# A two-layer mixer trunk on one core: gate and output projections of both mixers as seven block products, partners through DRAM

## The chip, the cores and the metric

One core of a Trainium2 chip runs the whole program. The metric is device time in microseconds of one execution; the time before is the median of three runs. In the profile TensorE is PE (its weight loads PEld), VectorE is DVE, ScalarE is ACT, GpSimd is POOL, SyncE is SP.

## What is computed

x is 1 × 1024 tokens × 1024 features, c one conditioning vector. Cut from the reference (layer 0 is gMLP, layer 1 retention, each followed by a squared-ReLU MLP):

```python
def spatial_gating_mixer(h, w_in, ln_g, ln_b, w_s, b_s, w_out):
    z = jax.nn.gelu(h @ w_in);  u, v = jnp.split(z, 2, axis=-1)        # 1024 -> 2 x 2048
    v = layer_norm(v, ln_g, ln_b).reshape(B, nc, CHUNK, SG_GROUPS, SG_GROUP_DIM)
    s = jnp.einsum('gtp,bnpgc->bntgc', jnp.tril(w_s), v) + b_s.T[:, :, None]   # chunks of 128 tokens
    return (u * s.reshape(B, S, SG_WIDTH)) @ w_out                     # 2048 -> 1024

def retention_mixer(h, w_in, gn_g, gn_b, w_out):                       # 4 heads, dk 256, dv 512
    q, k, v, g = jnp.split(h @ w_in, ...)                              # 1024, 1024, 2048, 2048
    o = chunkwise_retention(rotary(q), rotary(k) * RET_DK ** -0.5, v)  # a state per head, chunks of 128
    o = ((o - mu) * lax.rsqrt(var + 1e-5)) * gn_g + gn_b
    return (o * jax.nn.silu(g)) @ w_out                                # 2048 -> 1024

for i in range(2):
    mod = silu(c) @ ada_w[i] + ada_b[i]                                # shift, scale, gate for mixer and MLP
    h = rms_norm(x, pre_mix_g[i]) * (1 + scale_m) + shift_m
    x = x + gate_m * rms_norm(mixer(h), post_mix_g[i])
    h = rms_norm(x, pre_ffn_g[i]) * (1 + scale_f) + shift_f
    y = jnp.square(jax.nn.relu(h @ ffn_w_in[i])) @ ffn_w_out[i]        # 1024 -> 4096 -> 1024
    x = x + gate_f * rms_norm(y, post_ffn_g[i])
```

## The kernel before

The tokens are two streams a = 0, 1 of 512. h is kept feature-major (128 features × 512 tokens a tile, eight tiles a stream). Every operand is split into a high and a low part, `hi` + `lo`, and one product is three matmuls, hi·hi, hi·lo and lo·hi (`mm3`, L132 to L134). So each weight tile of 128 × 1024 costs ScalarE a cast (`hi`, L345) and VectorE a subtraction, the remainder (`lo`, L351); activations likewise.

Work is a list of items `It`, each with `fetch` (the weights' DMA on SP), `prep` (`hi` and `lo`) and `run` (24 matmuls of 512 columns, as a rule); single functions, the pieces, stand between items. The loop at the end of the file (`advance`) fetches and prepares up to AHEAD = 5 items ahead, as far as W_BUFS = 6 weight tiles and other caps let it; within that a scheduler sets each engine's order.

- `feat_items` (two items) makes 256 output features for one stream, `tok_items` (four items) 512 output features with tokens on partitions; `plain_items` and `out_items` are second factors for one stream, adding to `step.y` (`Step.add`, L727).
- `block_items` makes 256 features for **both** streams in seven products in place of eight (a 2 × 2 block scheme over the halves of the contraction, of the columns and the streams): per product 4 × 3 matmuls, 84 where plain takes 96. Its weights' sums are L458 to L463, the remainders L475, sums of the results L498. `seven_items` is the same for the second factor, per 512 rows of contraction 168 matmuls for 192, with weights' sums L594 to L600, remainders L613, and activations read back from DRAM (`zd`) and split (L558, L562). `Parts.put` makes the sums of activations for it (L527 to L530).
- `Ops` makes the streams' sums that the products of `block_items` need. Stream 0's h goes to DRAM (`hd`), stream 1's stays on chip; `sums` (L846 to L854) are spread over the eight items of stream 1's plain blocks.
- Only the two MLPs use this scheme (`ffn_items`): FIRST = 4 plain blocks of 16 for stream 0 and for stream 1, then 12 blocks in seven products, then the second factor. During the first stretch (eight items) the norm of the mixer's stream 1 runs as pieces: `Step.finish` loads, sums squares (L201) and multiplies by the gate (L749), updates x (L761), makes the factors; then the scaled rows (L781), the tiles' transposes (L225) and the affine to h (L698, L703, L704).
- The mixers go stream by stream: `sg_items(step, h)` makes v, its layer norm, then in turn u (`u_items`), the spatial product (`s_bg`, L1064, L1065: the high part against both parts of w_s in one matmul of 256 columns, the low part in one of 128; VectorE L1069 to L1071), and the output projection. `ret_items(step, h)` goes by heads: q, k, v, scores, then per chunk o, kv and an item of g; transposes of o, gate (L1240), projection.
- adaLN vectors are items too (`ada_items`: VectorE L287, L289), put between others by `spread`.

Of the kernel before, what the change touches and what calls it, by code (L numbers as in the profile page):

```python
# [8 lines left out]
F32 = mybir.dt.float32  # L9
# [4 lines left out]
P = 128  # L14
# [17 lines left out]
AHEAD = 5  # L32

# [23 lines left out]
def kernel(  # L57
# [200 lines left out]
    class It:  # L258
# [141 lines left out]
    def out_items(step, w, r0, zt, zahead=2):  # L400

        st, zp = {}, {}

        def zpre():
            for j in range(2):
                zp[j] = split2(zt[j], "zp")

        def fn(W, l, j):
            if j == 0:
                st["ps"] = [PW(), PW()]  # L410
            if j == 0:
# [14 lines left out]
        its[0].zpre, its[0].zahead = zpre, zahead
        return its

# [80 lines left out]
    class Parts:  # L509
# [6 lines left out]
        def __init__(self, key):  # L516
            self.key, self.seven, self.four = key, {}, {}

        def put(self, b, z1, z2):
# [14 lines left out]
            nc.gpsimd.dma_start(d[:, 5:7], sb)  # L534

# [30 lines left out]
    def seven_items(two, w, parts, pairs):  # L566
# [9 lines left out]
        def item(p, g):  # L576
# [66 lines left out]
            return It(run, fetch, (hi, lo), w=2, raw=raws, rel=2 * (p in (7, 4)), z=1, zrel=1, cap=OUT_CAP)  # L643
# [3 lines left out]
    def plain_items(step, w, parts, blocks):  # L647
# [4 lines left out]
        def fn(W, l, j):  # L652
# [12 lines left out]
            if l == 1:  # L665
                st.pop(("z", j))

# [13 lines left out]
    class H:  # L681
# [8 lines left out]
        def split(self, d, src, layer, ffn, first=False, keep=None):  # L690
# [8 lines left out]
            tmp = keep(d) if keep else G()  # L699
# [7 lines left out]
    class Step:  # L707
# [21 lines left out]
        def finish(self):  # L729
# [11 lines left out]
            def sums():  # L741
                ss = small(8)
                for t in range(NCH):
                    for l in range(2):
                        square_sum(y[t // 2, l][0][:, t % 2, :], ss[:, 2 * t + l : 2 * t + l + 1])
                for l in range(2):
                    for i in range(2):
                        yt = y[i, l][0]
                        nc.vector.tensor_tensor(  # L749
                            yt, yt, st["g"][:, l, :][:, None, :].broadcast_to([P, 2, 512]), ALU.mult  # L750
                        )
                st["r"] = row_rsqrt(row_mean(ss))
                st["ss"] = small(8)
# [21 lines left out]
            return [load, sums, update(0), update(1)] + ([] if self.ends else [factors])  # L775
# [12 lines left out]
    def reload(a, l, xs):  # L788

        for i in range(2):  # L790
            xs[i, l] = QH("xr")
            nc.sync.dma_start(xs[i, l], rows_of(xsrc[a], i, l))

# [6 lines left out]
    def reload_pieces(a, tile_):  # L800
# [756 lines left out]
```

## Time and profile before

| | |
|---|---|
| median of three runs | 2787.8 us (2787.01 to 2788.74) |
| the profiled execution | 2788.15 us, span 2786.4 us |
| TensorE busy | 2727.5 us (98%), 12360 matmuls and transposes |
| VectorE busy | 1835.2 us (66%) |
| ScalarE busy | 1236.6 us (44%) |
| GpSimd busy | 120.4 us (4%) |

Read it so: TensorE's share says that the time is made of matmuls; whether a matmul removed is time gained depends on whether its stretch has TensorE without gaps, so the next thing to read is the stretches, then the few rows in which TensorE waited and for whom.

### The profile page before, as it was taken

How to read it: one execution, taken by the hardware profiler on the slowest of the kernel's cores; microseconds unless marked ns; L12 is line 12 of the kernel's file. 1: busy time of each engine (PE TensorE's matmuls, PEld its weight loads, DVE VectorE, ACT ScalarE, POOL GpSimd, SP SyncE). 2: the span in 40 equal slices, each digit the busy share in tenths (PEclk: the TensorE clock that was granted, in tenths of full speed). 3: DMA queues.
4: the chain of work that ended last, by engine and by line, in shares of the span. 5: the costliest groups of instructions: out<-in, count | busy, mean ns of one | idle time of the engine just before them, and what ended most of it. 6: DMA issues, size and time to landing. Idle time of an engine off the chain costs nothing.

```text
span 2786.4 us, 32308 instructions
## 1 busy us (share of the span) xinstructions
PE 2727.5 (98%) x12360; PEld 2249.1 (81%) x12360; DVE 1835.2 (66%) x2459; ACT 1236.6 (44%) x1755; POOL 120.4 (4%) x206
## 2 busy tenths in 40 slices
PE   6999999999999999999999999999999999999997
PEld 5887878888887888887888888888888888888886
DVE  7775745677787777747655557655556766677745
ACT  4443433347555643344433335433427555564322
POOL 0000000001101000000000000000001001100000
PEclk9999999999999999999999999999999999999998
DMA  9632452256566554445213215323226545475433
GB/s 355 224 114 76 151 182 91 91 174 200 180 222 218 208 189 158 137 152 195 91 61 110 73 59 190 128 84 116 78 65 218 167 164 181 143 254 168 146 124 121
DMA packets 253419, 421.97 MB, mean 151 GB/s; under 512 B 14064, under 2 KB 113592, under 8 KB 253264
## 3 DMA queue, kind: packets, MB, share of 16 engines
q1 hardware_dynamic: 236816, 363.17, 39.9%
q0 software_dynamic: 16256, 56.67, 5.3%
q8 instruction: 97, 1.59, 0.2%
q14 instruction: 58, 0.48, 0.1%
q10 hardware_dynamic: 192, 0.07, 0.0%
HBM read 346.43 MB, written 73.42 MB: 151 GB/s over the span
## 4 chain that ended last, share of the span: by engine, by line
PE 87%; issue 6%; DVE 3%; DMA 2%; POOL 1%; ACT 1%; POOLq 0%; ACTq 0%; DVEq 0%; SPq 0%
PE ps L132 17%; PE ps L133 17%; PE ps L134 17%; PE pw L132 12%; PE pw L134 12%; PE pw L133 12%; DMA first<-in_ada_w_dram 1%; PE ps L225 1%; DVE w L351 1%; DMA raw<-in_sg_w_in_dram 1%; PE ps L1229 0%; DVE x L761 0%; DMA raw<-in_ada_w_dram 0%; DVE y L749 0%; PE ps L1064 0%
## 5 line engine op out<-in xcount | busy, mean ns | idle before, releaser
L132 PE MATMUL ps<-h,w 128*128 128x512 f32 x1696 | 664.7, 392 | 10.3 <-DVE g L1070 8.6
L134 PE MATMUL ps<-h,w 128*128 128x512 f32 x1696 | 663.8, 391 | 0.0
L133 PE MATMUL ps<-h,w 128*128 128x512 f32 x1696 | 663.3, 391 | 0.0
L351 DVE TENSOR_TENSOR w<-raw,w 128x1024 fp32r<-128x1024 f32 (+1 forms) x296 | 355.3, 1208 | 406.9 <-PE ps L133 164.4
L345 ACT CAST w<-raw 128x1024 fp32r<-128x1024 f32 (+1 forms) x296 | 303.9, 1035 | 569.5 <-PE pw L134 178.8
L132 PEld LDWEIGHTS ps<-h,w 128*128 128x128 f32 x1696 | 318.9, 188 | 79.5 <-issue 6.5
L133 PEld LDWEIGHTS ps<-h,w 128*128 128x128 f32 x1696 | 319.1, 188 | 67.5
L134 PEld LDWEIGHTS ps<-h,w 128*128 128x128 f32 x1696 | 318.8, 188 | 67.8
L132 PE MATMUL pw<-w,z 128*128 128x512 f32 x640 | 249.7, 390 | 0.0
L133 PE MATMUL pw<-w,z 128*128 128x512 f32 x640 | 249.0, 389 | 0.0
L134 PE MATMUL pw<-w,z 128*128 128x512 f32 x640 | 247.8, 389 | 0.0
L132 PE MATMUL pw<-w,zp 128*128 128x512 f32 x512 | 201.5, 394 | 0.0
L133 PE MATMUL pw<-w,zp 128*128 128x512 f32 x512 | 199.5, 390 | 0.2 <-DVE w L351 0.2
L134 PE MATMUL pw<-w,zp 128*128 128x512 f32 x512 | 198.4, 391 | 0.8 <-DVE zp L139 0.8
L613 DVE TENSOR_TENSOR w<-raw,w 128x1024 fp32r<-128x1024 f32 x84 | 102.8, 1223 | 89.3 <-issue 32.8
L558 ACT CAST z<-zraw 128x1024 fp32r<-128x1024 f32 x100 | 104.7, 1051 | 114.7 <-DVE z L562 91.2
L727 DVE TENSOR_TENSOR y<-y,pw 128x1024 f32<-128x1024 f32 x100 | 121.5, 1216 | 48.5 <-PE pw L134 48.5
L132 PEld LDWEIGHTS pw<-w,z 128*128 128x128 f32 x640 | 120.1, 188 | 26.2 <-DVE y L727 1.6
L134 PEld LDWEIGHTS pw<-w,z 128*128 128x128 f32 x640 | 120.2, 188 | 25.1
L133 PEld LDWEIGHTS pw<-w,z 128*128 128x128 f32 x640 | 120.2, 188 | 24.6
L608 ACT CAST w<-raw 128x1024 fp32r<-128x1024 f32 x84 | 88.2, 1051 | 114.6 <-PE pw L134 48.1
L562 DVE TENSOR_TENSOR z<-zraw,z 128x1024 fp32r<-128x1024 f32 x100 | 121.3, 1219 | 2.8 <-ACT z L558 2.8
(218 smaller groups left out, 4455.0 us busy)
## 6 DMA issues: line engine op xcount, KB each, us to landing
zraw<-zd SPq DMA_DIRECT2D x100, 512.0 KB, 4.4
raw<-in_ret_w_in_dram SPq DMA_DIRECT2D x92, 512.0 KB, 4.2
raw<-in_ada_w_dram SPq DMA_DIRECT2D x80, 512.0 KB, 6.6
raw<-in_ffn_w_in_dram SPq DMA_DIRECT2D x80, 512.0 KB, 4.5
raw<-in_ffn_w_out_dram SPq DMA_DIRECT2D x80, 512.0 KB, 5.5
raw<-in_sg_w_in_dram SPq DMA_DIRECT2D x68, 512.0 KB, 7.5
zd<-sz POOLq DMA_DIRECT2D x48, 512.0 KB, 5.0
raw<-in_sg_w_out_dram SPq DMA_DIRECT2D x32, 512.0 KB, 3.4
```

Of the source, the lines that this page charges most:

```text
L132: nc.tensor.matmul(ps, a.hi, b.hi, start=start, stop=False, skip_group_check=True)
L133: nc.tensor.matmul(ps, a.hi, b.lo, start=False, stop=False, skip_group_check=True)
L134: nc.tensor.matmul(ps, a.lo, b.hi, start=False, stop=stop, skip_group_check=True)
L225: nc.tensor.transpose(ps[:, t * P : (t + 1) * P], xs[t // 2, d // 4][:, t % 2, off : off + P], ident)
L345: nc.scalar.copy(st["w", key].hi, st["raw", key])
L351: nc.vector.tensor_tensor(W.lo, st.pop(("raw", key)), f(W.hi), ALU.subtract)
L558: nc.scalar.copy(st["z", key].hi, st["zraw", key])
L562: nc.vector.tensor_tensor(z.lo, st.pop(("zraw", key)), f(z.hi), ALU.subtract)
L608: nc.scalar.copy(st["w", p, g].hi, src)
L613: nc.vector.tensor_tensor(W.lo, st.pop(("src", p, g)), f(W.hi), ALU.subtract)
L727: nc.vector.tensor_tensor(y, y, ps, ALU.add)
```

## The change

FIRST goes from 4 to 2 blocks, and the two mixers get the scheme of the MLPs: u of gMLP (8 blocks, SG_FIRST = 4 of them plain), g of retention (8 blocks, 2 plain) and both output projections. One function, `wide_items`, does all four stages. So that all tokens are there:

- gMLP makes v of both streams first and keeps it in DRAM (`vd`); s is made per stream and goes to DRAM as the gate's partner (`sd`, class `Partner`), read back per block; the multiply is on VectorE.
- Retention goes by units (head, stream): the o, kv and transpose pieces of one unit stand between the q and k items of the next; normalized, transposed o goes to `sd` in 128 writes of 128 × 128, again read back per block.
- h of both streams goes to DRAM as well (64 writes), `Ops.load` reads eight tiles back, `Ops.sums(p)` makes one product's operands at a time, at items 1, 2 and 3 of four in stream 1's plain blocks (at 2, 4 and 6 of eight in gMLP).
- The norm chain has five positions in place of eight, its square sums and gate products come by output half; the first half's stand between the last items of the output projection.
- `seven_items` runs over groups of two pairs, and the last pair by itself.
- The spatial product is three matmuls of 128 columns per chunk and one VectorE operation of 512 columns per column tile.

```diff
+FIRST = 2
+SG_FIRST = 4
...
-            def sums():
-                ss = small(8)
+            def sums(l):
+                if l == 0:
+                    st["ys"] = small(8)
                 for t in range(NCH):
-                    for l in range(2):
-                        square_sum(y[t // 2, l][0][:, t % 2, :], ss[:, 2 * t + l : 2 * t + l + 1])
...
+            if early and l == 0 and j == 0:
+                step.pieces[0]()
+            if early and l == 0 and j == n - 1:
+                later(1, step.pieces[1])
...
+        def tile(self, a, xs, *ds, first=False):
+            for d in ds:
+                tmp = self.h[a].split(d, turned(xs, d), self.layer, self.ffn, first)
+                nc.gpsimd.dma_start(self.hd[:, a, d, :], tmp)
+
+        def load(self):
+            for kp in range(2):
+                for a in (1, 0):
+                    for half in range(2):
+                        t = self.s[a, half, kp] = QL("a", F32) if a and half else QH("a")
+                        k = half * 4 + kp * 2
+                        nc.sync.dma_start(t, self.hd[:, a, k : k + 2, :])
+
+        def sums(self, p):
+            for kp in range(2):
+                a11, a12, a21, a22 = (self.s[v, h, kp] for v in range(2) for h in range(2))
+                dst, x0, x1, op = {
+                    5: (a22, a21, a22, ALU.add), 6: (a22, a22, a11, ALU.subtract),
+                    7: (a11, a11, a21, ALU.subtract), 3: (a12, a12, a22, ALU.subtract),
+                }[p]
+                nc.vector.tensor_tensor(dst, x0, x1, op)
...
+    def wide_items(ops, two, wi, c0, wo, nb, first, act, partner, fore, pieces_a, pieces_b, pieces_o, mid=()):
...
+                if partner:
+                    nc.scalar.activation(r, src, act)
+                    fin = lambda: nc.vector.tensor_tensor(dst, halves(r), dst, ALU.mult)
...
+        its = weave(fore + gated(0), pieces_a)
+        its += weave(gated(1), pieces_b)
+        for n, b in enumerate(range(first, nb)):
+            its += weave(block(b), mid if n == 0 else ())
+        pairs = list(range(first // 2, nb // 2))
+        groups = [pairs[:-1][n : n + 2] for n in range(0, len(pairs) - 1, 2)] + [pairs[-1:]]
+        for g in groups:
+            its += seven_items(two, wo, parts, g)
+        return its + plain_items(two[0], wo, parts, list(range(first)), True) + weave(
+            plain_items(two[1], wo, parts, list(range(first))), pieces_o
+        )
...
+                for t in range(NCH):
+                    mm3(ps[:, t * P : (t + 1) * P], vn[t][:, j * P : (j + 1) * P], W, True, True)
+                nc.vector.scalar_tensor_tensor(v3(s), v3(ps), PR[:, R_LNG + ct : R_LNG + ct + 1], beta, ALU.mult, ALU.add)
+                nc.gpsimd.dma_start(sp.tokens(ct, a), s.rearrange("p (h c) -> p h c", h=2))
...
+            pieces = []
             for t in range(NCH):
+                pieces.append((t, lambda c_=c_, t=t: (c_["o"](t), c_["kv"](t))))
+                if t < NCH - 1:
+                    pieces.append((t + 1, lambda c_=c_, t=t: c_["turn"](t)))
...
+            its += nxt["pre"][:1] + weave(nxt["pre"][1:], pieces)
...
+        res = [
+            (0, lambda: (p[0](), p[1](), p[2]()) if whole else p[2]()),
+            (1, lambda: p[3]()),
+        ]
+                (2, lambda: (step.scaled(0), step.scaled(1))),
+                (3, lambda: to.tile(a, step.xs(), 0, 1, 2, 3)),
+                (4, lambda: to.tile(a, step.xs(), 4, 5, 6, 7)),
...
+    def sums(o, n):
+        k = n // 4
+        return [(0, o.load), (k, lambda: o.sums(5)), (2 * k, lambda: o.sums(6)), (3 * k, lambda: (o.sums(7), o.sums(3))), (n, o.last)]
```

Three places in the engines' orders. The first is TensorE's at gMLP's spatial product (ps are its sums, wsT the turned w_s, vn the normalized v), before and then now:

```order
L1064 MATMUL ps_1282<-wsT_730,vn_1121 128x256
L1065 MATMUL ps_1282<-wsT_730,vn_1122 128x128
L1064 MATMUL ps_1282<-wsT_730,vn_1121 128x256
L1065 MATMUL ps_1282<-wsT_730,vn_1122 128x128
L1064 MATMUL ps_1289<-wsT_730,vn_1128 128x256
L1065 MATMUL ps_1289<-wsT_730,vn_1129 128x128
```

```order
L134 MATMUL ps_1231<-wsT_1059,vn_1187 128x128
L135 MATMUL ps_1231<-wsT_1059,vn_1187 128x128
L136 MATMUL ps_1231<-wsT_1059,vn_1188 128x128
L134 MATMUL ps_1231<-wsT_1059,vn_1187 128x128
L135 MATMUL ps_1231<-wsT_1059,vn_1187 128x128
L136 MATMUL ps_1231<-wsT_1059,vn_1188 128x128
L134 MATMUL ps_1231<-wsT_1059,vn_1194 128x128
L135 MATMUL ps_1231<-wsT_1059,vn_1194 128x128
L136 MATMUL ps_1231<-wsT_1059,vn_1195 128x128
```

Two matmuls of two widths per chunk have become three of 128 columns (L134 to L136 are `mm3` in the changed file).

The second is TensorE's in the last stretch of an output projection, now: pw are sums of stream 1's plain items, y the scaled rows of stream 0, whose transposes are L227.

```order
L136 MATMUL pw_4777<-w_4766,z_4770 128x512
L227 MATMUL ps_4908<-ident,y_3901 128x128 x2
L227 MATMUL ps_4908<-ident,y_4163 128x128 x2
L227 MATMUL ps_4920<-ident,y_3901 128x128 x2
L227 MATMUL ps_4920<-ident,y_4163 128x128 x2
L227 MATMUL ps_4930<-ident,y_3901 128x128 x2
L227 MATMUL ps_4930<-ident,y_4163 128x128 x2
L227 MATMUL ps_4942<-ident,y_3901 128x128 x2
L227 MATMUL ps_4942<-ident,y_4163 128x128 x2
L134 MATMUL pw_4776<-w_4835,z_4838 128x512
```

Four tiles' transposes stand together behind three of the four items; before, they came by two or three at a time over eight items.

The third is VectorE's at the first MLP's first block products. Before (L846 to L854 are the operand sums, L351 weight remainders):

```order
L351 TENSOR_TENSOR w_5261<-raw_5029,w_5260 128x1024
L846 TENSOR_TENSOR s_1003_5409<-b_5119,b_5198 128x1024
L351 TENSOR_TENSOR w_5302<-raw_5079,w_5301 128x1024
L848 TENSOR_TENSOR b_5198<-s_1003_5409,a_5333 128x1024
L850 TENSOR_TENSOR a_5333<-a_5333,b_5119 128x1024
L852 TENSOR_TENSOR a_5335<-a_5335,b_5198 128x1024
L351 TENSOR_TENSOR w_5338<-raw_5134,w_5337 128x1024
L854 TENSOR_TENSOR h_5411<-s_1003_5409,h_5410 128x1024
```

Now (L808, L817 the operand sums and their remainders, L352 weight remainders, L447 the remainders of the first block's products):

```order
L808 TENSOR_TENSOR a_5469<-a_5469,a_5465 128x1024
L817 TENSOR_TENSOR h_5565<-a_5467,h_5564 128x1024
L817 TENSOR_TENSOR h_5569<-a_5475,h_5568 128x1024
L808 TENSOR_TENSOR a_5477<-a_5477,a_5473 128x1024
L808 TENSOR_TENSOR a_5471<-a_5471,a_5467 128x1024
L817 TENSOR_TENSOR h_5611<-a_5469,h_5610 128x1024
L817 TENSOR_TENSOR h_5615<-a_5477,h_5614 128x1024
L808 TENSOR_TENSOR a_5479<-a_5479,a_5475 128x1024
L432 TENSOR_TENSOR t_5578<-raw_5384,raw_5308 128x512
L447 TENSOR_TENSOR w_5580<-t_5578,w_5580 128x512
```

The operand sums stand in one run, and the second block product's weight remainder (w_5580) stands behind all of them.

## Rows read from the trace of the kernel before

**Rows 1.** The page: header, busy time by engine, DMA queues.
```profile
span 2786.4 us, 32308 instructions
PE 2727.5 (98%) x12360; PEld 2249.1 (81%) x12360; DVE 1835.2 (66%) x2459; ACT 1236.6 (44%) x1755; POOL 120.4 (4%) x206
...
q1 hardware_dynamic: 236816, 363.17, 39.9%
q0 software_dynamic: 16256, 56.67, 5.3%
```

**Rows 2.** Busy time by stretch: us, PE, PEld, DVE, ACT, POOL, granted clock, DMA.
```profile
770.00:840.00 70.00, 70.00 (x308) 57.37 (x307) 56.95 (x108) 39.94 (x70) 8.02 (x15) 1.00 0.65 216
980.00:1050.00 70.00, 70.00 (x310) 57.99 (x309) 49.96 (x47) 30.59 (x30) 0.00 (x0) 1.00 0.56 188
```

**Rows 3.** TensorE's timeline at the spatial product: start, duration.
```profile
448.62 0.22 PE L1065 MATMUL ps<-wsT,vn 128*128 128x128 f32 x1
448.68 0.33 PE L1064 MATMUL ps<-wsT,vn 128*128 128x256 f32 x1
448.85 0.22 PE L1065 MATMUL ps<-wsT,vn 128*128 128x128 f32 x1
```

**Rows 4.** TensorE's timeline at the scores, and that stretch's busy times.
```profile
1304.37 0.28 PE L132 MATMUL pw<-q,k 128*128 128x128 f32 x1
1304.48 0.27 PE L133 MATMUL pw<-q,k 128*128 128x128 f32 x1
...
1304.20:1304.90 0.70, 0.70 (x6) 0.70 (x7) 0.70 (x2) 0.01 (x1) 0.00 (x0) 1.00 0.97 342
```

**Rows 5.** The page's costliest groups, and VectorE's groups by form.
```profile
L132 PE MATMUL ps<-h,w 128*128 128x512 f32 x1696 | 664.7, 392 | 10.3 <-DVE g L1070 8.6
...
L1070 DVE SCALAR_TENSOR_TENSOR g<-ps,prm,g 128x256 f32<-128x256 f32 x64 | 29.2, 477 | 0.4
```

**Rows 6.** VectorE's timeline behind the last matmul.
```profile
2770.32 1.21 DVE L727 TENSOR_TENSOR y<-y,pw 128x1024 f32<-128x1024 f32 x1
2771.45 1.22 DVE L749 TENSOR_TENSOR y<-y,gg 128x1024 f32<-128x1024 f32 x1
```

**Rows 7.** VectorE's groups by form, mean ns of one.
```profile
L475 DVE TENSOR_TENSOR w<-raw,w 128x512 fp32r<-128x512 f32 x120 | 82.1, 689 | 56.5 <-ACT w L468 51.1 <-PE ps L133 5.2
L289 DVE SCALAR_TENSOR_TENSOR acc<-raw,cact,acc 128x512 f32<-128x512 f32 x140 | 105.4, 753 | 11.9 <-DMA raw<-in_ada_w_dram 10.1
L351 DVE TENSOR_TENSOR w<-raw,w 128x1024 fp32r<-128x1024 f32 x288 | 349.8, 1222 | 403.7 <-PE ps L133 161.2 <-PE pw L133 149.0 <-issue 77.9
```

**Rows 8.** Timelines of VectorE, ScalarE and TensorE in the norm of layer 0's mixer, stream 1.
```profile
626.59 1.21 DVE L727 TENSOR_TENSOR y<-y,pw 128x1024 f32<-128x1024 f32 x1
637.92 2.74 DVE L761 SCALAR_TENSOR_TENSOR x<-y,s,x 128x512 f32<-128x512 f32 x4 [1.52 <-POOL s L162]
...
647.02 0.72 ACT L781 ACTIVATE y<-x,rows 128x512 f32<-128x512 f32 x1 [0.82 <-POOL rows L162]
649.26 1.32 ACT L781 ACTIVATE y<-x,rows 128x512 f32<-128x512 f32 x2
...
653.58 1.03 PE L225 MATMUL ps<-ident,y 128*128 128x128 f32 x8
```

**Rows 9.** DMA issues: KB each, median us from issue to landing.
```profile
x<-xd SPq DMA_DIRECT2D x24, 512.0 KB, 3.8
hd<-g POOLq DMA_DIRECT2D x16, 256.0 KB, 4.2
```

**Rows 10.** Timelines of VectorE and TensorE around a retention state.
```profile
1331.58 1.23 DVE L139 TENSOR_TENSOR st<-state,st 128x1024 fp32r<-128x1024 f32 x1 [1.78 <-ACT st L138]
...
1333.24 0.39 PE L132 MATMUL ps<-st,q 128*128 128x512 f32 x1
```

**Rows 11.** Busy time by stretch, around a wait in gMLP.
```profile
255.00:259.00 4.00, 2.24 (x16) 1.95 (x15) 4.00 (x8) 0.46 (x1) 0.00 (x0) 1.00 0.00 0
259.00:262.50 3.50, 3.50 (x10) 2.71 (x9) 2.32 (x6) 1.04 (x1) 0.00 (x0) 0.51 0.08 9
```

More of the change, by code (lines that the diff above doesn't have):

```diff
@@ L642, in item, with plain_items @@
             raws = int(which is not None)
-            return It(run, fetch, (hi, lo), w=2, raw=raws, rel=2 * (p in (7, 4)), z=1, zrel=1, cap=OUT_CAP)
+            return It(run, fetch, (hi, lo), w=2, raw=raws, rel=2 * (p in (7, 4)), z=1, zrel=1, cap=OUT_CAP, ready=lambda: parts.whole(q),
+                      after=last == 0 and p in (5, 6))
         return [item(p, g) for p in ORDER for g in range(last + 1)]
-    def plain_items(step, w, parts, blocks):
+    def plain_items(step, w, parts, blocks, early=False):
         st = {}
@@ L993, in sg_prep, with sg_items, v_evac @@
                     )
-    def sg_items(step, h):
-        hh = lambda: h
-        wi, wo = sg_w_in[0], sg_w_out[0]
-        v, vn, u, ys = {}, {}, {}, {}
-        st = {}
-        def v_evac(cb):
+    def sg_items(ops, early):
+        wi = sg_w_in[0]
+        sp = Partner(SG_FIRST)
+        vd = [dram.tile([P, NCH, 2048], F32, tag=f"vd{a}", name=f"vd{a}") for a in range(2)]
+        st = [{}, {}]
+        def v_evac(a, cb):
             def evac(t, ps):
-                if "stats" not in st:
-                    st["stats"] = [
+                if "stats" not in st[a]:
+                    st[a]["stats"] = [
@@ new lines, in kv @@
+                if a == 1 and t == NCH - 1:
+                    return
+                s = rt["state"]
+                two = PW()
+                for kt in range(2):
+                    off = (t % 2) * 256 + kt * P
+                    mm3(two[:, kt, :], R["kd"][:, t // 2, off : off + P], R["v"][t], True, True)
+                if a == 0 and t == 0:
+                    nc.vector.tensor_copy(s, two)
+                else:
+                    nc.vector.scalar_tensor_tensor(s, s, GAMMA[hd] ** CH, two, ALU.mult, ALU.add)
@@ new lines, in run_wide @@
+    def run_wide(layer, ffn, o, wi, c0, wo, nb, first, act, partner, fore, pieces_a, to):
+        two = pair(layer, ffn)
+        for s_ in two:
+            s_.pieces = s_.finish()
+        return wide_items(
+            o, two, wi, c0, wo, nb, first, act, partner, fore, pieces_a, sums(o, 2 * first),
+            norm(two[0], to, False),
+        )
+    sg = run_wide(
+        0, False, ops[0], sg_w_in[0], 0, sg_w_out[0], 8, SG_FIRST, AF.Gelu_apprx_tanh, sp, [], rest, ops[1]
+    )
+    items += spread(g_its + sg, ada((0, 2), (0, 3), (0, 4), (0, 5)), 24, 90)
@@ new lines @@
+    f0 = run_wide(
+        0, True, ops[1], ffn_w_in[0], 0, ffn_w_out[0], 16, FIRST, None, None, [],
+        norm(steps[0, False, 1], ops[1], True), ops[2],
+    )
+    items += spread(f0, ada((1, 0), (1, 1)), 10, 80)
+    r_its, rp, rest = ret_items(ops[2], [(0, lambda: None)] + [(n + 1, p) for n, p in norm(steps[0, True, 1], ops[2], True)])
+    rw = run_wide(
+        1, False, ops[2], ret_w_in[0], 4096, ret_w_out[0], 8, FIRST, AF.Silu, rp, [], rest, ops[3]
+    )
+    items += spread(r_its + rw, ada((1, 2), (1, 3), (1, 4)), 8, 80)
```

608 lines of the change are left out of this document (253 added, 355 removed).

## The prediction

> **What bounds the kernel now.** I read the header and engine totals first [rows 1]: TensorE is busy 98% of the span, VectorE 66%, ScalarE 44%. So the time is the number of matmuls times their pitch, plus the places where TensorE waits. Second the stretches [rows 2]: 980:1050 holds 310 matmuls of 512 columns in 70.00 us, TensorE never idle, so one costs 70/310 = 0.226 us. The stretch 770:840 is block products of the MLP: VectorE is busy 56.95 of 70 us (81%) and TensorE still loses nothing. That decides what the same scheme may cost in the mixers: 80% VectorE hides.
>
> The profiled run is 2788.15 us, span 2786.4; the median of the runs shown is 2787.8, 0.35 less. I sum against 2788.15 and take 0.35 off at the end. About 0.2%, 5.6 us, can be told from no change.
>
> **The change, term by term.**
>
> *Matmuls saved.* The order of the two programs has 11420 matmuls of 512 columns before and 11084 now, 336 fewer: a block product takes 84 where plain takes 96 (12 saved), a pair of output blocks 168 for 192 (24 saved). MLPs, two more blocks each: 4×12 + 2×24 = 96; gMLP: 4×12 + 2×24 = 96; retention: 6×12 + 3×24 = 144. At 0.226 us: **−75.9**. TensorE was never idle where these lie, so all of it is on the path.
>
> *Spatial product.* Before, 128 pairs of a 256- and a 128-column matmul, 0.23 us from pair to pair (448.62 to 448.85) [rows 3], 29.4 us. Now 384 of 128 columns. The nearest rows of such a sequence, 128 behind 128, are the retention scores: 0.11 us from start to start at a granted clock of 1.00, with 7 weight loads busy for 0.70 of 0.70 us [rows 4]: a new stationary tile per matmul sets the pitch there, and the spatial product changes its tile from matmul to matmul too. So 42.2 us: **+12.8**. The other end: in [rows 3] the matmul behind a 128-column one starts 0.06 us later, and 384 × 0.06 = 23.0 would give −6.4. I take the rows of the same shape in the same sequence, and keep the other end.
>
> The Trainium skill ("TensorE: Matmul & The Clock Gate", Wait — 56ns, not 53.3ns?) says back-to-back matmuls of 128 columns start 55.6 ns apart once the array is warm. The scores' rows do not agree at the same clock; by the page this term would be 384 × 0.0556 − 29.4 = −8.0.
>
> *Its evacuations.* A column tile took four VectorE operations of 477 ns [rows 5]; now one of 512 columns. TensorE waited 8.6 us behind the last of them (the idle time of L132) [rows 5]. Most goes: **−6** (0 to −8.6).
>
> *Tail.* The last norm's square sums and gate products now come by output half, the first half's before the last matmuls. Two gate products (L749) that stand there before now, 1.13 us from start to start [rows 6], go: **−2.3**.
>
> *Costed at nothing:* gate products in place of squares move work from ScalarE (44%) to VectorE (see below). Partner and v transfers: by the order 304 more DMA issues on POOL (4% busy) and 61 more on SP, on queues at 5.3% and 39.9% [rows 1]; if they crowd, it shows as late operands, term 3 below.
>
> *New waits*, none of which the old trace shows as such; bounds from the nearest rows:
>
> 1. gMLP's four wide blocks. VectorE does 22 operations of 512 columns per block at 0.69 us (7 weight remainders, 4 weight sums, 3 evacuation sums, 4 partial sums, 4 gate products) [rows 7], 15.2 us in 84 × 0.226 = 19.0 us: 80% again. But the adaLN reductions of four vectors, 32 items of two operations of 0.753 us [rows 7], are spread over items 24 to 90, so a block of seven items has 32 × 7/66 = 3.4 of them (5.1 us): 20.3 in 19.0. Four blocks × 1.3 = 5, and 1 for the plain blocks ahead, which share the vectors and get the operand sums: **+6** (0, if work done ahead takes it up, to 25).
> 2. Norm of stream 1 at each stage's start, of stream 0 at its end. Before: last y add at 626.59, first x update 637.92, scaling from 647.02, the tiles' transposes at 653.58 [rows 8]: 27 us, with TensorE busy throughout. Now three items of 24 matmuls, 16.3 us, lie between the last add and the same transposes. Needed by then are the first four scalings, done at 650.5 (649.26 and two pipelined), 23.9 us behind the add; the half that is summed early takes two gate products (2.3) and four squares (4 × 0.66, as the scalings' two in 1.32) out: 19.0, or 2.7 late, six times 16 us. But half of ScalarE's time in those rows is other work, which can step back: I take 1 us each, **+6** (0 to 16).
> 3. The operands of the seven products. Before, stream 1's h stayed on chip, and the eight sums were woven into eight items (43 us). At the MLPs' starts there are now four items, 21.7 us, for: the write of h (4.2 us to landing), its reload (3.8 for a like one) [rows 9], and 16 VectorE operations of 1.22 us = 19.5 us, beside four items' weight remainders (4 × 1.22) and the first block's weights (5 × 0.69): 28 us of VectorE plus 8 of transfers against 21.7 plus the first product's 2.7. Behind the third pair of sums in VectorE's order stands the second product's weight remainder; TensorE waits for it. 28 + 8 − 24.4 = 12; the scheduler can put some remainders ahead, so 7.5 at each MLP, 3 at retention, where h has long been in DRAM: **+18** (0 to 60).
> 4. Groups of one pair at the end of every second factor, five of them: per product VectorE has a weight remainder, a z remainder and about 0.6 weight sums at 1.22 us and, like these, two y adds at 1.22, 5.6 us in all (4.6 × 1.22), against 24 × 0.226 = 5.4: 35 products: **+3** (0 to 8).
> 5. Retention. Before, the state's remainder was done at 1332.8 and used at 1333.24 [rows 10], 0.4 us of slack; the shape of the chain is kept, its cover is now q and k items with rotary work on VectorE: **+4** (0 to 10).
> 6. Clock. Waits cost twice: TensorE was busy 2.24 of 4 us in 255:259, and the next 3.5 us ran at a granted 0.51, the level of 1.2 GHz [rows 11], which loses 1.7. The two longest waits in (3) take 2.5 each as I judge, a little more than that one: **+5** (0 to 15).
>
> Together **+42**. Sum: 2788.15 − 75.9 + 12.8 − 6 − 2.3 + 42 = 2758.8; less 0.35: **2758 us**, 1.1% faster.
>
> On (3), the Trainium skill ("DMA: Bandwidth & Descriptors", Anatomy of one DMA — SWDGE (gpsimd) path) puts a fixed 2.0 us on every DMA, most of it the write's receipt, and bytes / 436e3 on top, and so speaks against the round trip. By it 256 KB takes 2.6 us and 512 KB 3.2, an estimate; the rows' 4.2 and 3.8 are longer, and the stage would wait 2.2 us less per start by the page.
>
> **Rivals.**
>
> *All hidden.* For: the 81% stretch of [rows 2] and the tiles' 27 us, which cost nothing; the scheduler can move remainders ahead of sums. Against: (3) is more VectorE work than its window. New waits of 0 to 20: 2716 to 2736, say 2726.
>
> *128-column matmuls at 0.06 us* [rows 3]: 384 × 0.05 = 19 us less than my sum, 2739. Against: [rows 4].
>
> *Slower: the sums unhidden.* If VectorE takes the sums only after the tiles are complete, TensorE stands for write, load and all 16 sums: 4.2 + 3.8 + 19.5 = 27.5 us at both MLPs and 19.5 at retention, 75 instead of 18, plus the clock at its bound, 10 more: 2758 + 57 + 10 = 2825. Without waits the sum is 2716.4, so it is slower than 2793.4 from 77 us of waits, that is some 20 us at each of the three starts with the rest as above. For: each sum in the order stands behind the tiles. Against: the plain products of stream 1 run meanwhile, 21.7 us.
>
> *It doesn't do what it says:* excluded, the order counts 336 fewer.
>
> **How the numbers follow.** My forecast (25 to 60 us of waits, 2741 to 2776): 0.55. All hidden: 0.25. Cheaper 128-column matmuls: 0.05. Waits of 60 to 77 us: 0.08, of which all of "within 0.2%" (2782.2 to 2793.4) comes. Slower: 0.07. Faster is 0.55 + 0.25 + 0.05 = 0.85. The range runs from 2716 (no wait) to 2790 (sums half hidden, 73 us of waits); outside lie the slower case, and a gain in the spatial product with everything hidden.
>
> **What would show it.** Right: TensorE's matmuls 336 fewer and its busy time down by about 60 us; gaps of 5 to 12 us ahead of the first block products of both MLPs, put down to VectorE at the sums or a weight remainder, with the granted clock near 0.5 behind them; short waits in gMLP's wide blocks with VectorE above 90%; 0.11 us between spatial matmuls. Wrong: those stretches with TensorE full (then 2726), or gaps over 20 us there, or large waits elsewhere, at POOL's or SP's transfers above all.

## The result, and the profile after

The changed kernel takes 2803.65 us (median of four runs, 2801.62 to 2805.58) where the kernel before took 2787.41: a ratio of 1.0058, 95% interval 1.0041 to 1.0076. It is slower by 16 us; 2758 was forecast, 30 us faster, with a range up to 2790. The direction was wrong.

The page of the changed kernel, the rows that answer to [rows 1] and to the matmul group of [rows 5]:

```profile
span 2801.9 us, 33485 instructions
PE 2694.4 (96%) x12152; PEld 2215.0 (79%) x12152; DVE 2018.3 (72%) x2697; ACT 1318.4 (47%) x1965; POOL 292.6 (10%) x510
...
L136 PE MATMUL ps<-h,w 128*128 128x512 f32 x1640 | 649.9, 397 | 25.2 <-DVE w L352 13.4
L134 PE MATMUL ps<-h,w 128*128 128x512 f32 x1640 | 649.3, 396 | 10.1 <-DVE g L685 8.8
```

TensorE is busy 33 us less, VectorE 183 us more, and the span is 15.5 us longer. The matmuls of the first factors (L134 to L136, `ps<-h,w`) now wait 35 us in all, 25.2 of them for a weight's remainder (13.4 at L352, the rest at L447, the remainders of block products); before, it was 10.3, none of it for a remainder.

TensorE's stretches of the changed kernel, columns as in [rows 2]. The four between 240 and 2220 in which it is not full are gMLP's spatial product and plain blocks (240:340), and the changes from mixer to MLP (560:720), from MLP to retention (1230:1370) and from retention to MLP (2080:2220):

```profile
0.00:240.00 240.00, 217.36 (x1064) 178.83 (x1065) 153.36 (x237) 106.86 (x155) 42.79 (x76) 1.00 0.76 262
240.00:340.00 100.00, 86.46 (x431) 73.10 (x430) 73.06 (x96) 33.79 (x44) 17.38 (x28) 0.88 0.75 254
340.00:560.00 220.00, 220.00 (x966) 180.90 (x965) 187.35 (x272) 99.74 (x137) 12.91 (x24) 1.00 0.69 238
560.00:720.00 160.00, 146.74 (x659) 119.43 (x658) 114.01 (x146) 90.30 (x160) 19.32 (x32) 0.98 0.59 203
720.00:1230.00 510.00, 510.00 (x2240) 420.46 (x2239) 373.06 (x485) 248.16 (x341) 27.85 (x52) 1.00 0.52 176
1230.00:1370.00 140.00, 122.07 (x558) 98.97 (x557) 102.26 (x136) 72.30 (x134) 18.94 (x29) 0.95 0.48 165
2080.00:2220.00 140.00, 119.48 (x518) 96.19 (x517) 103.47 (x129) 82.70 (x154) 19.45 (x29) 0.94 0.57 196
```

The same stretches before:

```profile
0.00:240.00 240.00, 212.75 (x958) 173.89 (x959) 174.09 (x308) 105.63 (x149) 8.30 (x15) 0.98 0.63 212
240.00:340.00 100.00, 97.66 (x469) 81.13 (x468) 70.57 (x94) 38.18 (x54) 0.00 (x0) 0.98 0.37 118
340.00:560.00 220.00, 213.86 (x970) 175.11 (x969) 126.35 (x174) 79.31 (x112) 3.02 (x3) 1.00 0.37 124
560.00:720.00 160.00, 159.43 (x755) 132.27 (x754) 123.23 (x156) 91.25 (x143) 14.70 (x25) 1.00 0.57 186
1230.00:1370.00 140.00, 137.55 (x636) 113.41 (x636) 93.45 (x127) 67.06 (x112) 7.15 (x8) 0.99 0.47 156
2080.00:2220.00 140.00, 139.57 (x651) 114.89 (x650) 101.81 (x124) 89.97 (x142) 15.76 (x27) 1.00 0.58 190
```

Lost time is span less busy time, and busy time × (1 − granted clock), here before → now, in us:

| stretch | idle | half clock | together, more than before |
|---|---|---|---|
| 0:240 | 27.3 → 22.6 | 4.3 → 0 | −8.9 |
| 240:340, spatial product | 2.3 → 13.5 | 2.0 → 10.4 | +19.6 |
| 340:560, gMLP's blocks | 6.1 → 0 | 0 → 0 | −6.1 |
| 560:720, to the first MLP | 0.6 → 13.3 | 0 → 2.9 | +15.6 |
| 1230:1370, to retention | 2.5 → 17.9 | 1.4 → 6.1 | +20.2 |
| 2080:2220, to the second MLP | 0.4 → 20.5 | 0 → 7.2 | +27.3 |
| near the end, 2773 | 0 → 3.25 | 0 → 1.46 | +4.7 |

That is 72 us. The span itself asks for 80: 15.5 more, where 63.1 less of matmuls (75.9 − 12.8, as forecast) and 1.4 less of tail (17.6 → 16.2 us behind the last matmul's start) should stand. The table sees too little: a matmul shows 0.39 us where its pitch is 0.23, so a gap is shown up to 0.16 short and a shorter one not at all. Counted from start to start instead, each step between two matmuls less the median step of their shapes, the waits come to 84 us more and the matmuls to 67 less. So the saved matmuls came in, to within some 4 us, and the waits were 80 us or a little more where the sum had 36 (42, less 6 for the old evacuations). Of the trace behind 240 us, TensorE stood idle 14.5 us before and 69.0 now, and up to the last matmul its clock was at half for 6.8 us before and 64.9 now.

The longest waits of TensorE in the changed kernel (start, duration, and in brackets the idle time and its releaser):

```profile
301.34 0.48 PE L134 MATMUL ps<-wsT,vn 128*128 128x128 f32 x1 [5.79 <-DVE g L1064]
...
689.32 0.80 PE L136 MATMUL ps<-h,w 128*128 128x512 f32 x1 [6.55 <-DVE w L447]
...
1262.63 0.47 PE L134 MATMUL pw<-w,z 128*128 128x512 f32 x1 [3.26 <-DVE s L209]
...
1304.16 0.79 PE L136 MATMUL ps<-h,w 128*128 128x512 f32 x1 [5.50 <-DVE w L352]
...
2143.01 0.79 PE L136 MATMUL ps<-h,w 128*128 128x512 f32 x1 [5.86 <-DVE w L352]
...
2200.71 0.79 PE L136 MATMUL ps<-h,w 128*128 128x512 f32 x1 [5.24 <-DVE w L447]
...
2773.49 0.76 PE L134 MATMUL pw<-w,z 128*128 128x512 f32 x1 [3.25 <-DVE y L709]
```

### The profile page after: what moved, and what is told of

Same layout as the page of the kernel before. It is cut to its first block, busy times and chain, and to the rows that moved or that the text cites. A ratio compares the mean times of both kernels' runs of the same rounds, so it can differ in the third digit from the quotient of the medians.

```text
span 2801.9 us, 33485 instructions
## 1 busy us (share of the span) xinstructions
PE 2694.4 (96%) x12152; PEld 2215.0 (79%) x12152; DVE 2018.3 (72%) x2697; ACT 1318.4 (47%) x1965; POOL 292.6 (10%) x510
## 5 line engine op out<-in xcount | busy, mean ns | idle before, releaser
L136 PE MATMUL ps<-h,w 128*128 128x512 f32 x1640 | 649.9, 397 | 25.2 <-DVE w L352 13.4
L134 PE MATMUL ps<-h,w 128*128 128x512 f32 x1640 | 649.3, 396 | 10.1 <-DVE g L685 8.8
L135 PE MATMUL ps<-h,w 128*128 128x512 f32 x1640 | 648.7, 396 | 0.0
L136 PEld LDWEIGHTS ps<-h,w 128*128 128x128 f32 x1640 | 312.4, 190 | 95.9 <-DVE w L352 15.1
L134 PEld LDWEIGHTS ps<-h,w 128*128 128x128 f32 x1640 | 312.3, 190 | 79.7 <-DVE g L685 9.8
L134 PE MATMUL pw<-w,z 128*128 128x512 f32 x928 | 362.9, 391 | 10.3 <-DVE s L209 6.4
L135 PEld LDWEIGHTS ps<-h,w 128*128 128x128 f32 x1640 | 312.1, 190 | 68.7
L135 PE MATMUL pw<-w,z 128*128 128x512 f32 x928 | 362.2, 390 | 2.8 <-DVE w L352 2.8
L136 PE MATMUL pw<-w,z 128*128 128x512 f32 x928 | 360.2, 390 | 0.0
L346 ACT CAST w<-raw 128x1024 fp32r<-128x1024 f32 x180 | 185.9, 1047 | 319.3 <-PE pw L136 90.8
L352 DVE TENSOR_TENSOR w<-raw,w 128x1024 fp32r<-128x1024 f32 x180 | 217.9, 1222 | 155.6 <-PE ps L135 73.5
L589 DVE TENSOR_TENSOR w<-raw,w 128x1024 fp32r<-128x1024 f32 x133 | 162.5, 1223 | 109.4 <-PE pw L135 45.1
L584 ACT CAST w<-raw 128x1024 fp32r<-128x1024 f32 x133 | 139.1, 1051 | 192.8 <-PE pw L136 75.9
L534 ACT CAST z<-zraw 128x1024 fp32r<-128x1024 f32 x153 | 159.5, 1050 | 140.2 <-DVE z L538 113.7
L134 PEld LDWEIGHTS pw<-w,z 128*128 128x128 f32 x928 | 174.7, 188 | 49.6 <-ACT g L203 7.2
L135 PEld LDWEIGHTS pw<-w,z 128*128 128x128 f32 x928 | 174.7, 188 | 39.4 <-DVE w L352 3.7
L136 PEld LDWEIGHTS pw<-w,z 128*128 128x128 f32 x928 | 174.5, 188 | 36.4
L538 DVE TENSOR_TENSOR z<-zraw,z 128x1024 fp32r<-128x1024 f32 x153 | 185.7, 1220 | 5.1 <-ACT z L534 5.0
L447 DVE TENSOR_TENSOR w<-raw,w 128x512 fp32r<-128x512 f32 x190 | 130.8, 690 | 74.9 <-ACT w L440 69.6
L135 PE MATMUL ps<-w,z 128*128 128x512 f32 x456 | 177.6, 390 | 0.0
L134 PE MATMUL ps<-w,z 128*128 128x512 f32 x456 | 177.6, 389 | 0.0
L136 PE MATMUL ps<-w,z 128*128 128x512 f32 x456 | 177.6, 389 | 0.0
```

What stands on the lines that cost most here:

```text
L134: nc.tensor.matmul(ps, a.hi, b.hi, start=start, stop=False, skip_group_check=True)
L135: nc.tensor.matmul(ps, a.hi, b.lo, start=False, stop=False, skip_group_check=True)
L136: nc.tensor.matmul(ps, a.lo, b.hi, start=False, stop=stop, skip_group_check=True)
L346: nc.scalar.copy(st["w", key].hi, st["raw", key])
L352: nc.vector.tensor_tensor(W.lo, st.pop(("raw", key)), f(W.hi), ALU.subtract)
L447: nc.vector.tensor_tensor(W.lo, st.pop(("src", p)), f(W.hi), ALU.subtract)
```

## What stands behind these waits

The waits were read backwards, from the releaser in the bracket to what stood ahead of it on its engine. Ahead of the second MLP, ScalarE's squares of stream 1's y wait for a buffer g, which the write of h to DRAM still holds (L789 issues that write, L203 wants the buffer):

```profile
2136.70 0.63 ACT L203 ACTIVATE g<-y 128x512 f32<-128x512 f32 x1 [4.12 <-DMA hd<-g]
```

and in VectorE's queue the gate products (L730) wait for these squares, the weight remainder (L352) for the gate products:

```profile
2138.07 3.68 DVE L730 TENSOR_TENSOR y<-y,gg 128x1024 f32<-128x1024 f32 x3 [2.86 <-ACT g L203]
...
2141.74 1.22 DVE L352 TENSOR_TENSOR w<-raw,w 128x1024 fp32r<-128x1024 f32 x1
```

TensorE stands for that remainder, 5.86 us at 2143.01. At 1262 it is y adds of stream 1 (L709), which free TensorE's accumulators, behind eight x updates of stream 0 in one piece (5.39 us); the bracket names the small operation right behind the add (L209):

```profile
1254.83 5.39 DVE L743 SCALAR_TENSOR_TENSOR x<-y,s,x 128x512 f32<-128x512 f32 x8 [1.15 <-POOL s L164]
1260.14 1.22 DVE L352 TENSOR_TENSOR w<-raw,w 128x1024 fp32r<-128x1024 f32 x1
1261.27 1.22 DVE L709 TENSOR_TENSOR y<-y,pw 128x1024 f32<-128x1024 f32 x1
```

At 2200 it is the run of operand sums that the third order excerpt showed for the first MLP, here the second's:

```profile
2198.24 1.22 DVE L808 TENSOR_TENSOR a<-a,a 128x1024 f32<-128x1024 f32 x1
2199.37 0.69 DVE L432 TENSOR_TENSOR t<-raw,raw 128x512 f32<-128x512 f32 x1
2199.97 0.69 DVE L447 TENSOR_TENSOR w<-t,w 128x512 fp32r<-128x512 f32 x1
```

and in gMLP an operand sum of stream 1's plain blocks waits 4.37 us for its reload, with the spatial product's evacuation, which has nothing to do with it, behind it:

```profile
299.40 1.23 DVE L808 TENSOR_TENSOR a<-a,a 128x1024 f32<-128x1024 f32 x1 [4.37 <-DMA a<-hd]
300.54 0.75 DVE L1064 SCALAR_TENSOR_TENSOR g<-ps,prm,beta 128x512 f32<-128x512 f32 x1
```

## Experiments

Three theories. **A**: norm chain and operand sums are packed into four items, and stand in VectorE's queue ahead of what TensorE needs; each wait is made in its own place. **B**: the writes of h hold the six buffers g. **C**: the operands' round trip through DRAM.

### e1: FIRST = 4

```diff
-FIRST = 2
+FIRST = 4
```

> FIRST back to 4 in both MLPs and retention, everything else as in the change (norm pieces still at positions 0 to 4, operand sums at items 2, 4, 6 of eight). 144 matmuls of 512 columns more, +32.5 us at 0.226. Theory A (the norm chain and the operand sums are packed into four items where VectorE, in order, needs more): the waits at the two MLPs' starts and at the ends of the second factors go, some 45 of the 70 us lost at the three stage changes: about 2791. Theory B (h's writes to DRAM hold the six buffers g, and ScalarE waits for them): those writes are the same, waits stay: about 2836. Theory C (DMA round trip of the operands): only the sums' waits of 6.5 and 5.2 us and their clock go: about 2820.

Measured: 2795.46 us (2794.44 to 2798.0), 8.2 less with 32.5 us more of matmuls, so 40.7 us of waits and half clock went. A, not B, and far more than C allows. The stretch that had 119.48 busy now has

```profile
2080.00:2220.00 140.00, 133.56 (x612) 108.88 (x611) 98.67 (x118) 82.86 (x144) 20.42 (x34) 1.00 0.68 233
```

### e2: FIRST = 4 and the norm over eight positions

```diff
-    norm(steps[0, False, 1], ops[1], True)
+    norm(steps[0, False, 1], ops[1], True, (0, 2, 4, 5, 7))
...
-    norm(two[0], to, False)
+    norm(two[0], to, False, (0, 2, 4, 5, 7))
```

(The tuple gives the item ahead of which each of the five pieces stands; the second MLP's start likewise.)

> As the kernel with FIRST = 4, and the norm's five pieces at positions 0, 2, 4, 5, 7 of eight at the MLPs' starts and at the ends of the second factors. Theory A: x updates and y adds no longer meet in VectorE's queue, 10 us less than the kernel with FIRST = 4 alone: about 2780. Theories B and C: no difference from it.

Measured: 2779.69 us (2777.4 to 2783.9), 15.8 less than e1, where A said 10. The matmuls are those of e1, and the kernel is now faster than the kernel before (ratio 0.9978, 0.9969 to 0.9988). ScalarE's waits for buffers held by writes of h are still 11.6 us in this trace (12.1 in the change), but they hardly reach TensorE any more; that speaks against B. The stretch is all but full:

```profile
2080.00:2220.00 140.00, 138.80 (x641) 114.23 (x640) 98.59 (x119) 86.49 (x150) 21.38 (x35) 1.00 0.70 237
```

### e3: eight buffers g

```diff
-QL_BUFS = 22
+QL_BUFS = 21
-G_BUFS = 6
+G_BUFS = 8
```

> The change with eight buffers g for six (and 21 for 22 of the large ones that pay for it). Theory B: ScalarE's waits behind h's writes go, and with them most of the waits at retention's and the second MLP's start: 25 to 35 us less, about 2774. Theory A: a few us, 2797 to 2803.

Measured: 2799.98 us (2797.09 to 2801.92), 3.7 less, inside A's range. That is hardly clear of noise: the ratios to the kernel before, 1.0051 (1.0035 to 1.0068) here and 1.0058 (1.0041 to 1.0076) for the change, overlap. Nor did two more buffers do what B asked: ScalarE still waits 10.7 us for writes of h, where it was 12.1, and the wait ahead of the second MLP is as long as it was:

```profile
2134.14 0.63 ACT L203 ACTIVATE g<-y 128x512 f32<-128x512 f32 x1 [4.43 <-DMA hd<-g]
```

So at 2139 TensorE still stands 5.01 us for the remainder, behind the gate products and these squares. This run doesn't separate A from B; e2 does, and e9 below, where no such wait is left and time is lost all the same.

### e4: gMLP's operand sums late

```diff
-        return [(0, o.load), (k, lambda: o.sums(5)), (2 * k, lambda: o.sums(6)), (3 * k, lambda: (o.sums(7), o.sums(3))), (n, o.last)]
+        return [(4, o.load), (6, lambda: o.sums(5)), (7, lambda: o.sums(6)), (8, lambda: (o.sums(7), o.sums(3))), (8, o.last)]
```

(The old line stays for the other stages; the new one is a second function, for gMLP alone; n is 8 there and k 2.)

> gMLP's operand loads at item 4 and sums at items 6, 7, 8 of eight, so that no operand sum stands ahead of an evacuation of the spatial product in VectorE's order. If the 24 us lost between 240 and 340 us come mostly from VectorE standing at the loads with the evacuations behind it (5.8 and 2.5 us, and the half clock after them): 10 to 14 us less, about 2791. If the sums are then late for the first block products: no difference, the wait moves to about 340 us.

Measured: 2790.4 us (2787.97 to 2792.84), 13.3 less; the waits of 5.79 and 2.46 us are gone, and the sums are not late for the blocks. The stretch lost 23.9 us in the change, 11.0 here (4.3 idle, 6.7 clock):

```profile
240.00:340.00 100.00, 95.71 (x486) 81.67 (x484) 72.51 (x105) 36.17 (x48) 18.46 (x30) 0.93 0.81 273
```

### e5 to e8: the gains together, and three finer cuts

e5 is e2 with e3's buffers and e4's positions.

> FIRST = 4 with the norm over eight positions, gMLP's operand sums late, and eight buffers g, the three gains of the first four runs together. Theory A (each wait is work packed into too few items or standing ahead in VectorE's queue, in its own place): the gains add: 2779.7 - 13 - 3.7 = about 2763, below both kernels. If they share one wait: 2770 to 2780.

Measured: 2771.4 us (2768.1 to 2771.67), 8.3 less than e2 and not 17: in the range of the second case. The traces show where the gains overlap. With the norm over eight positions the second MLP's start is all but full (e2), so more buffers g have nothing left to give there. And in 240:340 e2 lost 9.0 us of idle time and 13.7 of half clock, e5 loses 4.2 and 9.6, which is 8.9 less where e4 gained 13:

```profile
240.00:340.00 100.00, 95.82 (x471) 81.49 (x470) 69.63 (x102) 33.76 (x46) 18.45 (x30) 0.90 0.78 264
```

e6 moves the operand sums of the FIRST = 2 stages further into the first block:

```diff
+        return [(0, o.load), (2, lambda: o.sums(5)), (4, lambda: o.sums(6))]
...
+            mid=[(1, lambda: (o.sums(3), o.last())), (3, lambda: o.sums(7))]
```

> The change at FIRST = 2, with the operand sums of the MLPs and retention spread further: products 5 and 6 at items 2 and 4 of stream 1's plain blocks, those of products 3 and 7 inside the first block. Theory A: the waits ahead of the second product, 6.55 us at 689 and 5.24 us at 2200, mostly go, with the half clock after them: 2788 to 2793. Rival (VectorE's total between the tiles and the first block sets the time, whatever its order): the wait moves to the products 3 and 7, 2800 to 2804.

Measured: 2793.31 us (2792.15 to 2795.74), 10.3 less: the waits of 6.55 and 5.24 us fell to a few of about 1 us. The order, not the total, made these two.

e7 gives stream 1 the early half of the norm that the change gives stream 0 (`plain_items(two[1], ..., True)`, and `whole` false).

> The change at FIRST = 2, with the first half of stream 1's norm sums and gate products moved ahead of its last output items, as the change does for stream 0 alone. Theory A: the waits for a weight remainder behind stream 1's gate products and x updates (5.50 us at 1304, 5.86 us at 2143) shrink by half, and the tail by two gate products: 2792 to 2797. Rival: the same work then meets stream 0's norm in the last items, nothing gained: 2803.

Measured: 2802.41 us (2798.8 to 2805.73): no gain, the rival. The wait of 5.86 us ahead of the second MLP went, but those beside it grew, 2.63 us to 3.53 and 5.24 to 6.93, and the time at half clock grew from 64.9 to 68.3 us.

e8 is e5 with that early half.

> The kernel with FIRST = 4 and all three gains, and stream 1's first half sums early as well. If the early half helps at FIRST = 2 only because four items are too few, no difference from that kernel (2763) but the tail's 2 us: about 2761.

Measured: 2762.07 us (2759.47 to 2764.05), 9.3 less than e5, where 2 were expected (the 2761 was met by luck, since its base, e5, had come out 8 us higher than expected). With eight items the early half helps, with four it only moves the wait. Not all of the 9.3 need be its work: about 3 us are half clock at the spatial product, 20.5 us there in e5 and 13.7 here, which the edit doesn't touch. The tail is 16.2 us as in the change, so the 2 us expected of it did not come. Two of the stage changes are now full:

```profile
240.00:340.00 100.00, 93.62 (x474) 79.01 (x473) 68.70 (x100) 33.87 (x46) 18.45 (x30) 0.93 0.76 264
560.00:720.00 160.00, 160.00 (x734) 131.81 (x734) 113.62 (x140) 97.74 (x168) 21.57 (x36) 1.00 0.65 220
1230.00:1370.00 140.00, 131.80 (x633) 107.78 (x632) 100.74 (x138) 67.59 (x112) 22.23 (x38) 0.99 0.50 166
2080.00:2220.00 140.00, 140.00 (x646) 115.41 (x645) 97.29 (x120) 83.84 (x139) 20.87 (x37) 1.00 0.65 219
```

### e9 to e12: the parts of the change apart

e9 is the kernel **before** with `FIRST = 2` (and the grouping of pairs that this needs, with the order of fetches and remainders for a last pair by itself), mixers as they were.

> The kernel before with FIRST = 2 and nothing else of the change (the last pair of the second factor by itself, as the change has it; mixers as before). 96 matmuls fewer, -21.7 us. Theory A (FIRST = 2 alone makes the stage starts too short for norm and sums): the saving is lost to waits at the two MLPs' starts, 2780 to 2795. Rival (the waits come from the mixers' new form): 2765 to 2768.

Measured: 2797.01 us (2795.55 to 2798.97), 10.2 slower than the kernel before in the same set (2786.82), with 21.7 us less of matmuls: 32 us of new waits and half clock without any of the mixers' new form, and without a wait for a buffer held by a write of h. Here it is the norm chain itself that comes late: the longest waits are those of the transposes of stream 1's tiles at both MLPs (3.76 us at 657 and again at 2168), behind the tiles' affine on VectorE:

```profile
657.48 1.84 PE L225 MATMUL ps<-ident,y 128*128 128x128 f32 x8 [3.76 <-DVE b L708]
```

e10 is the change at FIRST = 2 with e3, e4 and e6.

> The change at FIRST = 2 with all repairs that need no more items: gMLP's sums late (-13), operand sums into the first block (-10), eight buffers g (-4). Theory A, gains add: about 2776, still 14 above the best kernel with FIRST = 4 although that has 144 matmuls (32.5 us) more. If FIRST = 2 is not the cause of what is left: 2762 or below.

Measured: 2779.41 us (2772.92 to 2782.9), as A says: 8.0 more than e5, which has 144 matmuls more.

e11 is e8 with retention alone at 2 plain blocks.

> The best kernel so far (FIRST = 4, all gains, 2762) with retention alone at 2 plain blocks: 48 matmuls fewer, -10.8 us; its stage end then has four items for stream 0's norm, which lost 6 us and some half clock in the change. Theory A: 2758 to 2764. Rival (stage ends cost nothing): 2751.

Measured: 2765.35 us (2761.88 to 2765.65), 3.3 more than e8 with 10.8 us less of matmuls; about 14 us of waits and half clock came with it, a little over A. Some 5 us of that are half clock at the spatial product (23.9 us there, 13.7 in e8), which the edit doesn't touch, so retention's share is about 9 us, near the 10.8 saved.

e12 is e8 with the spatial product of the kernel before:

```diff
-                for t in range(NCH):
-                    mm3(ps[:, t * P : (t + 1) * P], vn[t][:, j * P : (j + 1) * P], W, True, True)
...
+                            nc.tensor.matmul(ps[:, o_ : o_ + 2 * P], vt.hi, w, start=True, stop=False)
+                            nc.tensor.matmul(ps[:, o_ : o_ + P], vt.lo, w[:, :P], start=False, stop=True)
```

> The best kernel so far with the spatial product of the kernel before: per chunk a matmul of 256 and one of 128 columns, and four VectorE operations of 256 columns per column tile. If the new form costs what its 0.11 us per matmul of 128 columns says (42.2 against 29.4 us) and VectorE has room: about 2751. If VectorE is the bound there (96 operations more, some 37 us of it less 24 us): 2760 to 2770.

Measured: 2745.39 us (2744.07 to 2747.07), 16.7 less than e8, where 11 was said: the new form of the product costs its matmuls and brought nothing back. VectorE has 23 us more to do in this stretch, and TensorE lost less there (93.62 busy at 0.93 in e8, above):

```profile
240.00:340.00 100.00, 95.35 (x456) 77.54 (x456) 91.67 (x155) 39.62 (x52) 17.34 (x29) 0.97 0.83 286
```

The pitch is again that of [rows 3], 0.23 us a pair:

```profile
249.58 0.22 PE L1066 MATMUL ps<-wsT,vn 128*128 128x128 f32 x1
249.63 0.34 PE L1065 MATMUL ps<-wsT,vn 128*128 128x256 f32 x1
249.81 0.22 PE L1066 MATMUL ps<-wsT,vn 128*128 128x128 f32 x1
```

e12 is the fastest of all: 0.9855 of the kernel before (0.9841 to 0.9870). It closes the account, too: 192 matmuls fewer at 0.226 are 43.4 us, 2786.8 − 43.4 = 2743.4, and 2745.4 was measured, so that its waits are about those of the kernel before (15.3 us of idle behind 240 us, where that had 14.5).

## Why the prediction was wrong, point by point

- **Matmuls saved, −75.9**: right to within some 4 us. Every stretch without norms or operand sums is full (340:560, 720:1230 with 510.00 of 510.00 us busy), and e12's sum closes within 2 us.
- **Spatial product, +12.8**: right, by the rows of the scores. In the changed kernel it runs at 0.11 us:

```profile
249.81 0.28 PE L135 MATMUL ps<-wsT,vn 128*128 128x128 f32 x1
249.93 0.27 PE L134 MATMUL ps<-wsT,vn 128*128 128x128 f32 x1
```

Every matmul has a weight load of its own (12152 of both in the page of the profile), and a pitch set by that load fits the rows: three matmuls a chunk cost three times 0.11, and the old pair twice 0.11 (0.23), though its first one has 256 columns. The Trainium skill's figure for back-to-back matmuls of 128 columns ("TensorE: Matmul & The Clock Gate", Wait — 56ns, not 53.3ns?: 55.6 ns once warm) is half of what these rows show.
- **Its evacuations, −6**: wrong in sign. The 8.6 us of waits behind the four operations went, and 10.0 us of waits behind the new one came, most of them from operand sums ahead of it in VectorE's queue, with half clock behind them (e4, which moves the sums: 13.3 us). I had read what waited there before, and not what the order of the change puts in front.
- **Tail, −2.3**: 1.4. Two of four gate products did go from behind the last matmul, but what the tail is made of there is the last y add (2787.22), then ScalarE's squares of its result, for which VectorE waits 1.46 us, and only then the last gate product (2789.89); the term took the gate products alone. The x updates of stream 0 in one piece ahead of stream 1's y adds cost 3.25 us at 2773 besides.
- **Wide blocks of gMLP, +6**: 0, at 187.35 of 220 us of VectorE (85%) in 340:560. A stretch of one block's length, 19.0 us, holds 17.3 us of VectorE where the sum had 20.3, and no gap of TensorE:

```profile
400.00:419.00 19.00, 19.00 (x85) 15.59 (x84) 17.34 (x37) 8.68 (x15) 1.89 (x4) 1.00 0.79 258
```

The adaLN work does lie there. The sum took an operation at the time that its row shows, 0.69 us, but one behind the other they start 0.60 us apart (2199.37 and 2199.97 above); the tail's term had used starts.
- **Norm, +6**: this is the step that failed. The brackets of TensorE's waits put about 40 us to it: 7 around the first MLP's start, 15 at retention's, 15 at the second MLP's, 3 near the end. About 12 of them are what the step had priced, matmuls and transposes behind the tiles' affine (L685); the other 27 it put at nothing: 16 for weight remainders (L352) and 10 for y adds (L709, with L209), the rest for work of retention's. The step asked only when the tiles' scalings would be ready for their transposes, found 2.7 us each, and halved that because ScalarE's other work "can step back". It did not ask what stands behind the chain's parts in VectorE's queue: weight remainders and y adds, for which TensorE waits while the tiles are not yet due. e1, e2 and e9 show that the four items are the cause: 41 us of waits and half clock go with eight (the sums' 12 among them), 16 more with the pieces spread over them, and 32 come to the kernel before with four. In e9 they come by the step's own question, tiles that are late, and even so cost 5 to 7 us of idle time at each of three stage starts, not 1 us.
- **Operand sums, +18**: 11.8 us of waits (6.55 + 5.24), nothing at retention; the size was fair, and e6 shows the place. The transfers came out longer than the rows of before had them (4.2 and 3.8 us); at both MLPs seven of the eight reloads are sent off within some 3 us, but no run shows that this is the reason. The Trainium skill's 2.0 us + bytes / 436e3, which it gives for transfers by GpSimd's path ("DMA: Bandwidth & Descriptors", Anatomy of one DMA — SWDGE (gpsimd) path), makes an estimate of 2.6 us for the writes, less than half of what they took; the reloads, for which the prediction worked out 3.2 by it too, go by SyncE's queue and took 9.5 (the median of the four that the trace times). Issues of the changed kernel, as [rows 9]:

```profile
hd<-g POOLq DMA_DIRECT2D x64, 256.0 KB, 5.6
...
a<-hd SPq DMA_DIRECT2D x32, 512.0 KB, 9.5
```

- **Single-pair groups, +3**: 0 (720:1230 is full); at 1.13 us from start to start (2198.24 to 2199.37 above), and not 1.22, its 4.6 operations are 5.2 us, under the 5.4 of a product's matmuls. **Retention, +4**: 3.4, at 1349, where the scores' split of the first unit is late.
- **Clock, +5**: 28 us lost to half clock by the table where the kernel before lost 8: +20. Six of the seven listed waits, all but the one at 1262, have a stretch at half clock behind them (rows for 689, 1304 and 2773 in the last section), not only the two longest, and so have some of the shorter ones, such as 2.38 us at 256 in the spatial product.
- The rival on the slow side was the sums unhidden at 20 us a start; it has the side right, its threshold of 77 us of waits is close to the 80 by luck, and the mechanism is wrong: the sums were 12 us of it.

The 11 us that e4 leaves at 240:340 are waits of 0.96, 2.25 and 0.87 us (248, 255 and 276) and 13.7 us at half clock, of which 10.2 begin at the wait of 2.25 us for normalized v. What is not settled: why so long a stretch at half clock follows that wait; and whether retention's start, which still lost 8.2 us in e8, can be spread, since no run tried it.

## What to carry to other kernels

A matmul removed is time gained only if what hid behind it has another cover: halving a stage's plain items took away the window of a norm chain that did not shrink. When a chain on an in-order engine is packed closer, price it by what is queued behind each waiting part and who waits for that, and not only by when the chain's own result is due: here the first was 27 us and the second 12. Where two sizes of a block are free to choose (FIRST 2 or 4), a smaller number of matmuls and a longer window are to be weighed by one run each: here 32.5 us of matmuls bought 41 us. A sum over an engine's work takes the time from start to start, not the time that a row shows for one operation.

## What the runs showed that was not expected

The stretches behind four of the waits (two for that of 6.55 us, then those of 3.26, 5.50 and 3.25 us):

```profile
689.30:692.70 3.40, 3.38 (x8) 2.71 (x9) 3.40 (x6) 2.81 (x5) 0.00 (x0) 0.50 0.53 164
692.70:696.10 3.40, 3.40 (x12) 2.70 (x12) 3.40 (x5) 1.37 (x3) 0.00 (x0) 0.75 0.43 147
1262.60:1265.80 3.20, 3.17 (x14) 2.68 (x15) 2.30 (x3) 0.26 (x2) 1.91 (x1) 1.00 0.55 179
1304.10:1307.50 3.40, 3.34 (x8) 2.66 (x9) 2.40 (x6) 1.61 (x4) 1.50 (x1) 0.50 0.91 288
2773.40:2776.40 3.00, 2.91 (x7) 2.36 (x8) 3.00 (x3) 2.56 (x8) 0.00 (x0) 0.50 0.05 21
```

The granted clock is 0.50, the level of 1.2 GHz, behind the wait of 3.25 us at 2773 as behind the long ones; behind the equally long one at 1262 it stayed at 1.00. It lasted 5.1 us behind the wait of 6.55 us (to 694.4, the middle of the second stretch), in which 12 matmuls start 0.43 us apart and not 0.23, some 2.4 us lost; 3.0 us behind the one of 3.25, 7 matmuls, some 1.4 us lost. So several middling waits cost more than their sum, by an amount that their length alone does not tell. The second surprise is the spatial product: at 0.11 us per matmul and weight load, a matmul of 256 columns cost no more than one of 128 in these rows (a pair of both 0.23 us), and the old form with its four evacuations for one was the faster by 16.7 us in an otherwise equal kernel (e12 against e8).
